# Moving the matmul operands of a transformer trunk to one address residue, and three smaller edits at its two ends

## The chip, the cores and the metric

The kernel runs on one core of one Trainium2 chip. The metric is the device time of one execution in microseconds (us). Three timed runs of the kernel before gave 1330.05, 1331.74 and 1331.91 us, median 1331.74 us.

## The reference

One layer of a hybrid encoder on 256 tokens of width 2048, all in float32:

```python
def reference(x, ...):                                   # x (1, 256, 2048)
    h = rms_norm(x, norm_mix); proj = h @ w_in            # (256, 9216): uv | q,k,v | two gates
    y_a = gmlp_branch(uv, ln_g, ln_b, w_s, b_s)           # u * (w_s @ layer_norm(v) + b), 8 groups
    y_b = neighbourhood_attn(q, k, v, rpb)                # 16 heads, windows of 4 rows x 16 columns
    merged = sigmoid(g_a) * (y_a @ w_branch[:1024]) + sigmoid(g_b) * (y_b @ w_branch[1024:])
    x = x + merged @ w_out
    up = rms_norm(x, norm_ffn) @ w_up                     # (256, 2 * 5504)
    up = conv3_over_tokens(up, conv_k) + conv_b
    gate, val = split(up)
    x = x + (silu(gate) * val) @ w_down
    return rms_norm(x, norm_final)
```

Almost all of the work is in five products with weights: `w_in`, `w_branch`, `w_out`, `w_up`, `w_down`.

## The kernel before

**Products in two halves.** Every float32 operand of a large product is held as two tiles of the type float32r: a high part (a rounded copy, written by ScalarE) and a low part (the rest, written by VectorE). A product is the sum of three: high x high, low x high, high x low. So one weight piece, a raw tile `wraw` of 128 x 1024, becomes a *unit*, the tiles `whi` and `wlo` (helpers `high`, L245, and `low`, L248). The activations are kept in the same way: `h` (the normalised input, later the normalised second input), `y` (the two branches), `m` (the merge), `a` and `s` (the activations of the down projection, and sums of them).

**A stream of pieces.** The weights lie in HBM in the order of use. `load` keeps up to five raw tiles under way (four slots of another shape, `start`, for the first 16 pieces, which carry 256 columns of the transposed x beside 1024 of weights). `begin(i)` is called ahead of every piece: it issues loads, lets `prepare` split pieces up to four ahead as units come free (`queue`, in order), and then runs the tasks that were put down for that piece with `at(i, f)`. Each engine works in the order in which this was written out.

**Which operand is loaded and which streams.** A matmul has a stationary operand (128 columns, put in by a weight load, the rows on PEld) and a moving one. There are four kinds of step:

- `first_step` (L381 to L384), the first 16 pieces: activations stationary, 512 columns of weights moving.
- `nat_step` (L364 to L366, through `three_products`): the same, for `va`, the gates, the branches and `w_out`.
- `wide_step` (L364 to L366): the down projection, 1024 columns a piece. Of its tiles three pairs in each group go through seven products in place of eight (sums of weights, made on VectorE, L301 to L304).
- `ws_step`, "ws" for weight-stationary (`spread_products`, L349 and L355), for u, q/k and the up projection: the weights are stationary. With a high weight tile, 512 columns move (both halves of 256 tokens, L349); with a low one, 256 columns (the high half alone, L355). Even pieces take highs and then lows, odd pieces lows and then highs, so that on TensorE runs of 16 highs and 16 lows alternate.

**Where tiles lie.** Pools on the left side of a partition's memory are stacked from the bottom: `const`, then `weights` (raw tiles, units 0 to 3), `tmp`, `hT` (the `h` tiles) and pools of a stage. Pools on the right are stacked from the top: `y`, the second input `x`, and `seven`, which adds units 4 and 5 and a half unit once the out projection has begun. All these tiles are multiples of 256 bytes long, so each side has one residue of its addresses modulo 256. As the kernel is built, that is 0 on the left and 224 on the right. Taking each large matmul's moving operand against the stationary operand of the next matmul in the program, 3346 of the 512-column float32r matmuls have the same residue, and 1329 differ by 32 bytes modulo 256 (the highs of units 4 and 5 in the up projection; all steps with `y`; the down steps whose weights lie in unit 4, unit 5 or the half unit). Of the 256-column ones, the lows of `ws_step`, 1304 have the same residue and 455 differ so.

**The start.** `load` is called ahead of the load of `gmix`, the scale of the first norm. Piece 0 comes in three transfers: its x columns on ScalarE's queue, its two weight halves on SP's. TensorE runs 14 transposes of an identity (`keep_awake`, L561), until the first data are there.

**The end.** In the last down group, `by_block` is 4: the four last pieces are multiplied block by block at the group's last step, so that the four blocks of the output end one after the other. The sums of the seven-product pairs are combined by `combine`, in the three tasks `one`, `two` and `three` at the pieces i + 1, i + 2 and i + 3 after the last pair.

Of the kernel before, what the change touches and what calls it, by code (L numbers as in the profile page):

```python
# [8 lines left out]
F32 = mybir.dt.float32  # L9
F32R = mybir.dt.float32r  # L10
# [5 lines left out]
T = 256  # L16
D = 2048
NT = T // 128
KD = D // 128
# [20 lines left out]
BLOCK = 1024  # L40
AHEAD = 5
RAW, UNITS, HALVES = 5, (4, 2), 1
WAKE = 14
EARLY = 4

FF_BLOCKS = ((0, 22), (22, 43))
FF_SEVEN = ((3, 5, 7), (2, 4, 6))
# [71 lines left out]
def weight_pieces():  # L119

    groups, order = weight_stream()
    out, count, at = [], {}, 0
    for key in order:
        _, w, pieces = groups[key]
        tiles, blocks = pieces[count.get(key, 0)]
        count[key] = count.get(key, 0) + 1
        cols = sum(n for _, n in blocks)
        out.append((key, w, tiles, blocks, at, cols))
        at += 128 * len(tiles) * cols
    return out, at  # L130
# [19 lines left out]
def trunk_kernel(ctx, tc, x, weights, vectors, ln_g, ln_b, w_s_turned, b_s, rpb, norm_final, out):  # L150
    nc = tc.nc
# [18 lines left out]
    ypool, y_st = pool("yT", "right")  # L170

    junk = tmp.tile([128, 512], F32, name="junk")

    banks = {n: None for n in range(8)}
    spare = list(range(8))

    def bank():
        n = spare.pop(0)
        banks[n] = psum.tile([128, 512], F32, name=f"bank{n}")
        return banks[n]  # L180
# [7 lines left out]
    pieces, _ = weight_pieces()  # L188
    kinds = {key: g[0] for key, g in weight_stream()[0].items()}
# [16 lines left out]
    def at(i, f):  # L206
        tasks.setdefault(i, []).append(f)
# [5 lines left out]
    def load():  # L213
        while n_loaded[0] < len(pieces):
            i = n_loaded[0]
            slots = start_free if i < KD else raw_free
            if not slots:
                return
            n_loaded[0] += 1
            for f in preload.pop(i, ()):  # L220
                f()
            _, _, tiles, _, off, cols = pieces[i]
            size = len(tiles) * cols
            slot = slots.pop(0)
            w = slot[0].tile([128, size if i < KD else BLOCK], F32, name=slot[1])
            for c0, c1 in ((T, 768), (0, T), (768, 1280)) if i == 0 else ((0, size),):
                queue = nc.scalar if (i, c0) == (0, 0) else nc.sync
                queue.dma_start(w[:, c0:c1], bass.AP(tensor=weights.tensor, offset=weights.offset + off + c0,
                                                       ap=[[size, 128], [1, c1 - c0]]))
            raw[i] = (w, slot)  # L230

    def raw_done(i):
        (start_free if i < KD else raw_free).append(raw.pop(i)[1])

    def unit(key):
        slot = unit_free.pop(0)
        h, l = (slot[0].tile([128, BLOCK], F32R, name=f"w{p}{slot[1]}") for p in ("hi", "lo"))
        units[key] = (h, l, slot)
        return h, l

    def unit_done(key):
        unit_free.append(units.pop(key)[2])

    def high(h, w):
        nc.scalar.activation(h, w, AF.Copy)  # L245

    def low(l, w, h):
        nc.vector.tensor_sub(l, w, h.bitcast(F32))  # L248

    def split_first(i):  # L250
        def go():
# [6 lines left out]
            else:  # L258
                nc.scalar.activation(dst[:, 0, :], x, AF.Copy, scale=g)
            nc.vector.scalar_tensor_tensor(dst[:, 1, :], x, g, dst[:, 0, :].bitcast(F32), op0=OP.mult,  # L260
                                           op1=OP.subtract)
            parts = ((0, 512), (512, 1024)) if i < EARLY else ((0, 1024),)
            for c0, c1 in parts:
# [5 lines left out]
    def split_piece(i):  # L269
        if i < KD:  # L270
            return split_first(i)

        def go():
            size = len(pieces[i][2]) * pieces[i][5]
            h, l = unit(i)
            w = raw[i][0]
            high(h[:, :size], w[:, :size])
            low(l[:, :size], w[:, :size], h[:, :size])
            raw_done(i)
        return go  # L280
# [38 lines left out]
    queue = []  # L319
# [104 lines left out]
    def wide_step(key, acts, sevens, rest, done, by_block=0):  # L424


        n0, size = starts[key], size_of[key]
        tiles = [pieces[n0 + n][2][0] for n in range(size)]
        firsts = [n for n in range(size) if n0 + n in seven]
        box, opened, left = {}, set(), {}  # L430
        OUT = {(0, 0): 2, (0, 1): 3, (1, 0): 4, (1, 1): 8}
        uses = []
        n = 0
        while n < size:
            if n in firsts:
# [12 lines left out]

        def product(u, x, w):
            start = u not in opened  # L450
            opened.add(u)
            left[u] -= 1
            three_products(p(u), x, w, start, left[u] == 0)

        def combine(i):

            nu, nv = (fx["p"].tile([128, 512], F32, name=f"comb{n}") for n in range(2))

            def one():
                nc.scalar.activation(nu, p(1), AF.Copy)  # L460
                rest(0, 0, nu, OP.add)
                nc.vector.tensor_sub(nu, nu, p(6))
                nc.vector.tensor_sub(nv, nu, p(7))
                free(p(1), p(6), p(7))

            def two():
                rest(0, 1, nu, OP.subtract)
                rest(0, 1, p(5), OP.add)
                rest(1, 0, nv, OP.add)

            def three():
                rest(1, 1, nv, OP.subtract)
                rest(1, 1, p(5), OP.add)
                free(p(5))

            for n, f in enumerate((one, two, three)):
                at(i + 1 + n, f)

        def step(i):
            n = i - n0  # L480
            c0, c1 = slice(0, 512), slice(512, 1024)
            if n in firsts:
                k = tiles[n]
                h, l, _ = halves[i]
                hb, lb, _ = units[i, "b"]
                product(1, acts(k, 0), (h, l))
                product(2, acts(k + 1, 0), (hb[:, c0], lb[:, c0]))
                product(3, sevens(k)[3], (hb[:, c1], lb[:, c1]))
                half_free.append(halves.pop(i)[2])
                unit_done((i, "b"))  # L490
            elif n - 1 in firsts:
                k = tiles[n - 1]
                ht, lt, _ = units[i - 1, "t"]
                hs, ls, _ = units[i - 1, "s"]
                S = sevens(k)
                product(5, S[0], (ht[:, c0], lt[:, c0]))
                product(7, S[2], (ht[:, c1], lt[:, c1]))
                unit_done((i - 1, "t"))
                product(6, S[1], (hs[:, c1], ls[:, c1]))
                product(4, acts(k + 1, 1), (hs[:, c0], ls[:, c0]))  # L500
                unit_done((i - 1, "s"))
                if n - 1 == firsts[-1]:
                    combine(i)
            elif n < size - by_block:
                h, l, _ = units[i]
                for (b, c), u in OUT.items():
                    cs = slice(c * 512, (c + 1) * 512)
                    product(u, acts(tiles[n], b), (h[:, cs], l[:, cs]))
                unit_done(i)
            elif n == size - 1:  # L510
                for b, c in ((0, 0), (1, 0), (0, 1), (1, 1)):
                    u = OUT[b, c]
                    for m in range(size - by_block, size):
                        h, l, _ = units[n0 + m]
                        cs = slice(c * 512, (c + 1) * 512)
                        product(u, acts(tiles[m], b), (h[:, cs], l[:, cs]))
                    done(p(u), b, c, i + 1)
                    free(p(u))
                for m in range(size - by_block, size):
# [24 lines left out]
    vec = const.tile([128, 2 * KD + 8 * NF], F32)  # L544
    gmix, gffn = vec[:, :KD], vec[:, KD:2 * KD]
    ck = vec[:, 2 * KD:].rearrange("p (j f) -> p j f", j=4)
    load()
    nc.scalar.dma_start(gmix, vectors[:, :KD])

    one = const.tile([128, 1], F32)  # L550
    nc.vector.memset(one, 1.0)
# [10 lines left out]

    keep_awake(WAKE)
    free(wake)
# [588 lines left out]
    for n in range(len(FF_BLOCKS)):  # L1153
        for j in range(2):
            key = ("down", n, j)
# [110 lines left out]
    for i, piece in enumerate(pieces):  # L1266
        key = piece[0]
# [45 lines left out]
```

## Time and profile before

| what | value |
|---|---|
| median of three timed runs | 1331.74 us |
| the profiled execution, its own time | 1331.57 us |
| span of its instructions | 1329.1 us |
| mean granted TensorE clock | 0.998 |
| TensorE busy | 1316.1 us, 99% of the span |
| VectorE busy | 71% |
| ScalarE busy | 55% |
| HBM traffic over the span | 194 GB/s |

A row of the page's groups gives the line, engine and operation, the tiles written and read without their numbers, the count, the busy time and the mean duration of one. Durations of matmuls overlap (a matmul is under way while the one before it drains), so the pace is read from the distance of two starts in the timeline, and the mean durations serve only to compare one group with another. In the timeline a row is the start, the time to the end, and what was run; "x16" are sixteen instructions of one kind in a row.

### The profile page before, as it was taken

The page shows a single profiled execution, that of the slowest core. Times are in us where ns is not written, and L with a number is a line of the kernel's source. Part 1 is how long each engine was busy: PE and PEld are TensorE (multiplying, and loading weights), DVE is VectorE, ACT ScalarE, POOL GpSimd, SP SyncE. Part 2 cuts the span into 40 slices and gives each one's busy share as a digit, 9 for nine tenths or more (in the row PEclk, how much of TensorE's full clock was granted, in tenths as well). Part 3 has the DMA queues.
Part 4 walks back from the last instruction along what each step waited for, and adds up shares of the span by engine and source line. Part 5 has one row for each costly group of instructions (what it writes and reads, how often), then busy time and mean ns, then how long its engine had stood idle before and what let it go on. Part 6 is the DMA issues. An engine that isn't in the chain of part 4 may idle for free.

```text
span 1329.1 us, 18475 instructions
## 1 busy us (share of the span) xinstructions
PE 1316.1 (99%) x6778; PEld 1116.5 (84%) x6778; DVE 945.4 (71%) x1362; ACT 728.8 (55%) x1072; POOL 100.3 (8%) x192
## 2 busy tenths in 40 slices
PE   9999999999999999999999999999999999999996
PEld 7888888888788888888888888888888888888885
DVE  5676667776564546565878777797858787869986
ACT  5855567576444444454655555554545555546553
POOL 0502065430000000000000000000000000000000
PEclk9999999999999999999999999999999999999999
DMA  8857676655556667665565656556656565546743
GB/s 327 321 177 208 195 218 191 203 151 190 180 182 189 190 189 255 204 189 187 171 203 174 200 179 199 180 175 220 207 190 190 191 187 194 183 135 222 249 147 127
DMA packets 73898, 261.40 MB, mean 197 GB/s; under 512 B 9552, under 2 KB 10832, under 8 KB 73296
## 3 DMA queue, kind: packets, MB, share of 16 engines
q1 hardware_dynamic: 69696, 252.33, 59.0%
q0 software_dynamic: 3680, 7.30, 2.0%
q8 instruction: 53, 0.87, 0.3%
q10 hardware_dynamic: 432, 0.60, 0.1%
q14 instruction: 37, 0.30, 0.1%
HBM read 256.00 MB, written 2.10 MB: 194 GB/s over the span
## 4 chain that ended last, share of the span: by engine, by line
PE 95%; DVE 3%; DMA 1%; ACT 1%; issue 0%; ACTq 0%; DVEq 0%
PE bank L349 30%; PE bank L355 16%; PE bank L364 14%; PE bank L366 14%; PE bank L365 14%; PE bank L381 1%; PE bank L382 1%; PE bank L384 1%; DVE wlo L248 1%; DMA wraw<-in_weights_dram 1%; PE bank L830 1%; ACT whi L245 0%; PE bank L882 0%; DMA vec<-in_vectors_dram 0%; PE bank L704 0%
## 5 line engine op out<-in xcount | busy, mean ns | idle before, releaser
L248 DVE TENSOR_TENSOR wlo<-wraw,whi 128x1024 fp32r<-128x1024 f32 (+1 forms) x466 | 561.2, 1217 | 231.1 <-ACT whi L245 223.5
L245 ACT ACTIVATE whi<-wraw 128x1024 fp32r<-128x1024 f32 (+1 forms) x466 | 481.1, 1046 | 285.2 <-PE bank L365 168.9
L349 PE MATMUL bank<-h,whi 128*128 128x512 f32 x1760 | 425.8, 392 | 0.0
L349 PEld LDWEIGHTS bank<-h,whi 128*128 128x128 f32 x1760 | 322.2, 188 | 64.1
L355 PEld LDWEIGHTS bank<-h,wlo 128*128 128x128 f32 x1760 | 225.3, 190 | 9.4
L355 PE MATMUL bank<-h,wlo 128*128 128x256 f32 x1760 | 229.5, 282 | 0.0
L364 PE MATMUL bank<-whi,h 128*128 128x512 f32 x320 | 126.0, 394 | 0.0
L366 PE MATMUL bank<-wlo,h 128*128 128x512 f32 x320 | 124.8, 390 | 0.0
L365 PE MATMUL bank<-whi,h 128*128 128x512 f32 x320 | 124.6, 389 | 0.0
L366 PE MATMUL bank<-wlo,a 128*128 128x512 f32 x248 | 97.2, 392 | 0.8 <-DVE wlo L248 0.8
L364 PE MATMUL bank<-whi,a 128*128 128x512 f32 x248 | 97.2, 392 | 0.0
L365 PE MATMUL bank<-whi,a 128*128 128x512 f32 x248 | 97.2, 392 | 0.0
L1020 ACT ACTIVATE tc<-ta,vec 128x256 f32<-128x256 f32 x86 | 47.1, 595 | 84.4 <-DVE ta L1018 84.4
L696 DVE TENSOR_TENSOR ta<-bank,tb 128x256 f32<-128x256 f32 x110 | 39.0, 417 | 67.6 <-ACT tb L694 67.6
L694 ACT ACTIVATE tb<-bank 128x256 f32<-128x256 f32 x110 | 36.2, 384 | 90.9 <-PE bank L349 86.2
L366 PEld LDWEIGHTS bank<-wlo,h 128*128 128x128 f32 x320 | 60.1, 188 | 12.8
L364 PEld LDWEIGHTS bank<-whi,h 128*128 128x128 f32 x320 | 60.1, 188 | 12.3
L365 PEld LDWEIGHTS bank<-whi,h 128*128 128x128 f32 x320 | 60.1, 188 | 12.0
L366 PEld LDWEIGHTS bank<-wlo,a 128*128 128x128 f32 x248 | 46.6, 188 | 11.6 <-DVE wlo L248 1.3
L364 PEld LDWEIGHTS bank<-whi,a 128*128 128x128 f32 x248 | 46.6, 188 | 10.3
L365 PEld LDWEIGHTS bank<-whi,a 128*128 128x128 f32 x248 | 46.6, 188 | 10.3
L1260 POOL DMA_DIRECT2D h<-in_norm_final_dram x4 | 2.2, 539 | 680.0 <-DVE wlo L248 679.5
(182 smaller groups left out, 1465.8 us busy)
## 6 DMA issues: line engine op xcount, KB each, us to landing
wraw<-in_weights_dram SPq DMA_DIRECT2D x446, 512.0 KB, 4.3
start<-in_weights_dram SPq DMA_DIRECT2D x15, 640.0 KB, 6.5
xs<-in_x_dram SPq DMA_DIRECT2D x2, 1024.0 KB, 9.5
vw<-va POOLq DMA_DIRECT2D x32, 64.0 KB, 5.3
x<-in_x_dram POOLq DMA_DIRECT2D x2, 1024.0 KB, 9.3
wraw<-in_weights_dram SPq DMA_DIRECT2D x8, 256.0 KB, 2.9
run<-in_rpb_dram POOLq DMA_DIRECT2D x64, 31.2 KB, 4.2
out_dram<-x SPq DMA_DIRECT2D x5, 256.0 KB, 2.8
```

The costliest lines, as they stand in the source:

```text
L245: nc.scalar.activation(h, w, AF.Copy)
L248: nc.vector.tensor_sub(l, w, h.bitcast(F32))
L349: nc.tensor.matmul(p, h[:, c:c + 128], acts(2 * n + k), start=n == 0 and k == 0, stop=last and k == tiles - 1)
L355: nc.tensor.matmul(p[:, :T], l[:, c:c + 128], acts(2 * n + k)[:, 0, :], start=False, stop=False)
L364: nc.tensor.matmul(p, xh, wh, start=start, stop=False)
L365: nc.tensor.matmul(p, xl, wh, start=False, stop=False)
L366: nc.tensor.matmul(p, xh, wl, start=False, stop=stop)
L381: nc.tensor.matmul(p, xh, h[:, cs], start=n == 0, stop=False)
L382: nc.tensor.matmul(p, xl, h[:, cs], start=False, stop=False)
L694: nc.scalar.activation(t, p[:, T:], AF.Copy)
L696: nc.vector.tensor_add(a, p[:, :T], t)
L1020: nc.scalar.activation(v, u, AF.Identity, scale=ck[:, 1, ch:ch + 1], bias=ck[:, 3, ch:ch + 1])
```

## The change

- A tile `line` of 56 floats (224 bytes) is added to `const`. It is never written or read; it moves all left pools up by 224 bytes.
- The tile `wlo` of a unit is 64 floats longer. In the weight-stationary steps the low part begins 8 floats (32 bytes) into it, in the others at its start.
- As built, all the operands of the large products lie at 224 modulo 256, and the lows of the weight-stationary steps at 0. Of the 512-column matmuls 4562 now have the same residue as the next stationary operand and 113 differ by 32 bytes; of the 256-column ones 120 and 1639. Because of the longer `wlo`, the residues modulo 512 are now mixed: 2318 of the 512-column matmuls have a stationary operand of their own that lies 256 bytes off modulo 512. Before there was no such pair.
- The load of `gmix` is issued ahead of `load`. Pieces 0, 1 and 2 come in two transfers each, columns 0 to 768 (x and the first weight half) and 768 to 1280, all on SP's queue.
- 18 transposes instead of 14 at the start.
- In the group with `by_block` the three tasks of `combine` run together at piece i + 3.

```diff
-WAKE = 14
+WAKE = 18
 EARLY = 4
+SPLIT = 3
+LINE = 64
+LOW_AT = 8
...
+    const.tile([128, 56], F32, name="line")
...
-            for c0, c1 in ((T, 768), (0, T), (768, 1280)) if i == 0 else ((0, size),):
-                queue = nc.scalar if (i, c0) == (0, 0) else nc.sync
-                queue.dma_start(w[:, c0:c1], ...)
+            for c0, c1 in ((0, 768), (768, 1280)) if i < SPLIT else ((0, size),):
+                nc.sync.dma_start(w[:, c0:c1], ...)
...
-    def unit(key):
+    def unit(key, low_at=0):
         slot = unit_free.pop(0)
-        h, l = (slot[0].tile([128, BLOCK], F32R, name=f"w{p}{slot[1]}") for p in ("hi", "lo"))
+        h = slot[0].tile([128, BLOCK], F32R, name=f"whi{slot[1]}")
+        l = slot[0].tile([128, BLOCK + LINE], F32R, name=f"wlo{slot[1]}")[:, low_at:low_at + BLOCK]
...
-            size = len(pieces[i][2]) * pieces[i][5]
-            h, l = unit(i)
+            size, key = len(pieces[i][2]) * pieces[i][5], pieces[i][0]
+            h, l = unit(i, LOW_AT if kinds[key] == "ws" else 0)
...
-                at(i + 1 + n, f)
+                at(i + 3 if by_block else i + 1 + n, f)
...
-    load()
     nc.scalar.dma_start(gmix, vectors[:, :KD])
+    load()
```

The order of TensorE's instructions is the same but for the four transposes. Two places move. On SP's queue, at the very start, these stood before (`start` are the raw tiles of the first pieces; 128x512 are the two weight halves of piece 0):

```order
L228 DMA start_86<-in_weights_dram 128x512 x2
L228 DMA start_90<-in_weights_dram 128x1280
L228 DMA start_92<-in_weights_dram 128x1280
L228 DMA start_94<-in_weights_dram 128x1280
L228 DMA start_205<-in_weights_dram 128x1280
```

and these stand there now:

```order
L231 DMA start_88<-in_weights_dram 128x768
L231 DMA start_88<-in_weights_dram 128x512
L231 DMA start_91<-in_weights_dram 128x768
L231 DMA start_91<-in_weights_dram 128x512
L231 DMA start_94<-in_weights_dram 128x768
L231 DMA start_94<-in_weights_dram 128x512
L231 DMA start_97<-in_weights_dram 128x1280
```

The x columns of piece 0 have come over from ScalarE's queue, and the first three pieces are six transfers. On VectorE, in the last down group, from the low part of the third-last piece on, these stood before (`x` is the residual that takes the result, `comb` the scratch tiles of `combine`):

```order
L248 TENSOR_TENSOR wlo_12126<-wraw_12072,whi_12125 128x1024
L958 TENSOR_TENSOR x_4961<-x_4961,comb_12123 128x512
L462 TENSOR_TENSOR comb_12123<-comb_12123,bank_11962 128x512
L463 TENSOR_TENSOR comb_12124<-comb_12123,bank_11958 128x512
L248 TENSOR_TENSOR wlo_12146<-wraw_12074,whi_12145 128x1024
L958 TENSOR_TENSOR x_4961<-x_4961,comb_12123 128x512
L958 TENSOR_TENSOR x_4961<-x_4961,bank_11954 128x512
L958 TENSOR_TENSOR x_4961<-x_4961,comb_12124 128x512
L248 TENSOR_TENSOR wlo_12165<-wraw_12092,whi_12164 128x1024
L958 TENSOR_TENSOR x_4961<-x_4961,comb_12124 128x512
L958 TENSOR_TENSOR x_4961<-x_4961,bank_11954 128x512
L964 TENSOR_TENSOR x_4961<-bank_11848,x_4961 128x512
```

and these stand there now:

```order
L252 TENSOR_TENSOR wlo_12132<-wraw_12078,whi_12131 128x1024
L252 TENSOR_TENSOR wlo_12148<-wraw_12080,whi_12147 128x1024
L252 TENSOR_TENSOR wlo_12164<-wraw_12098,whi_12163 128x1024
L962 TENSOR_TENSOR x_4967<-x_4967,comb_12129 128x512
L466 TENSOR_TENSOR comb_12129<-comb_12129,bank_11968 128x512
L467 TENSOR_TENSOR comb_12130<-comb_12129,bank_11964 128x512
L962 TENSOR_TENSOR x_4967<-x_4967,comb_12129 128x512
L962 TENSOR_TENSOR x_4967<-x_4967,bank_11960 128x512
L962 TENSOR_TENSOR x_4967<-x_4967,comb_12130 128x512 x2
L962 TENSOR_TENSOR x_4967<-x_4967,bank_11960 128x512
L968 TENSOR_TENSOR x_4967<-bank_11854,x_4967 128x512
```

The low parts of the last two pieces now stand ahead of all eight operations of `combine`, where they stood among them. ScalarE's copy for `combine` (L460) moves behind the high parts of these pieces in the same way.

More of the change, by code (lines that the diff above doesn't have):

```diff
@@ L225, in load @@
             w = slot[0].tile([128, size if i < KD else BLOCK], F32, name=slot[1])
-            for c0, c1 in ((T, 768), (0, T), (768, 1280)) if i == 0 else ((0, size),):
-                queue = nc.scalar if (i, c0) == (0, 0) else nc.sync
-                queue.dma_start(w[:, c0:c1], bass.AP(tensor=weights.tensor, offset=weights.offset + off + c0,
+            for c0, c1 in ((0, 768), (768, 1280)) if i < SPLIT else ((0, size),):
+                nc.sync.dma_start(w[:, c0:c1], bass.AP(tensor=weights.tensor, offset=weights.offset + off + c0,
                                                        ap=[[size, 128], [1, c1 - c0]]))
@@ L546, in trunk_kernel @@
     ck = vec[:, 2 * KD:].rearrange("p (j f) -> p j f", j=4)
+    nc.scalar.dma_start(gmix, vectors[:, :KD])
     load()
-    nc.scalar.dma_start(gmix, vectors[:, :KD])
     one = const.tile([128, 1], F32)
```

## The prediction

> **What bounds the kernel now.** The page's head and busy times come first, then the chain of work that ended last.
>
> ```profile
> span 1329.1 us, 18475 instructions
> PE 1316.1 (99%) x6778; PEld 1116.5 (84%) x6778; DVE 945.4 (71%) x1362; ACT 728.8 (55%) x1072; POOL 100.3 (8%) x192
> ...
> PE 95%; DVE 3%; DMA 1%; ACT 1%; issue 0%; ACTq 0%; DVEq 0%
> ```
>
> TensorE (PE) is busy 99% of the span and carries 95% of the chain. So the time is the number of matmuls times their pace, and only what changes the pace, or lies at the start and the end, can count. The pace hangs on where the operands lie. In the window from 390 to 450 us the groups by line have products with `h` (left, both operands at residue 0) beside products with `y` (right, at 224); the last two figures but one are busy time and mean duration in ns:
>
> ```profile
> L365 PE MATMUL bank<-whi,h 128*128 128x512 f32 x55 | 21.4, 389 | 0.0
> L364 PE MATMUL bank<-whi,y 128*128 128x512 f32 x32 | 12.6, 395 | 0.0
> ```
>
> In a down step the sides are exchanged (activations left, weights left or right). The timeline of the last group: piece 15 lies in a left unit, piece 16, from about 1304.3, in a right one.
>
> ```profile
> 1301.80 0.39 PE L365 MATMUL bank<-whi,a 128*128 128x512 f32 x1
> ...
> 1304.52 0.40 PE L365 MATMUL bank<-whi,a 128*128 128x512 f32 x1
> ...
> 1307.32 0.40 PE L365 MATMUL bank<-whi,a 128*128 128x512 f32 x1
> ```
>
> By the distance of starts twelve matmuls take 2.72 us, then twelve take 2.80: 226.7 and 233.3 ns. The third place is the up projection, where only the unit changes within one group:
>
> ```profile
> 702.42 3.82 PE L349 MATMUL bank<-h,whi 128*128 128x512 f32 x16
> 706.08 2.05 PE L355 MATMUL bank<-h,wlo 128*128 128x256 f32 x16
> 707.96 3.90 PE L349 MATMUL bank<-h,whi 128*128 128x512 f32 x16
> 711.70 2.06 PE L355 MATMUL bank<-h,wlo 128*128 128x256 f32 x16
> 713.59 3.82 PE L349 MATMUL bank<-h,whi 128*128 128x512 f32 x16
> 717.24 2.08 PE L355 MATMUL bank<-h,wlo 128*128 128x256 f32 x16
> 719.16 3.82 PE L349 MATMUL bank<-h,whi 128*128 128x512 f32 x16
> ```
>
> The highs at 702.42 and 713.59 are in units 0 to 3 and take 3.66 and 3.65 us by their starts; those at 707.96 are in units 4 and 5 and take 3.74. For the lows it is the other way round: 16 in left units take 1.92 us (717.24 to 719.16); where 8 of the 16 are in a right unit, 1.88 and 1.89. So 32 bytes between the moving operand and the loaded one cost a 512-column matmul 5 to 7 ns, and save a 256-column one some 3 ns (0.025 us for 8, taking 1.91 for the sixteen). The change takes the first away and spreads the second.
>
> **The sum, part by part**, against the profiled execution: 1331.57 us, of which 1329.1 is the span; that is 0.17 us under the median shown.
>
> *Gates, branches, out and down (L364 to L366).* Mixed today are 384 matmuls with `y` (4 column blocks x 2 branches x 8 tiles x 2 token blocks x 3) and 480 in right units. At 226.7 for 233.3 ns that would be 5.7 us; by the mean durations (6 ns) 5.2. I take **-5.4**.
>
> *Up projection.* Six pieces, one turn through the six units, last 719.16 - 702.42 = 16.74 us. After: highs 3.66 three times, plus 6 ns each for the last high of a run, since a low unit is loaded next; lows with all 16 off by 32 bytes: 16 save 0.05 less the last one, 1.865. Three times 5.53 is 16.59. The 176 pieces are 29.3 turns of 0.15: **-4.4**.
>
> *u and q/k.* All four units there are at 0. 48 pieces are 24 pairs, of which each gains 0.047 and pays 0.006: **-1.0**.
>
> *The end.* PE waits in the last group for the low part of the last piece, which stands behind six of the eight operations of `combine`:
>
> ```profile
> 1303.02 1.23 DVE L248 TENSOR_TENSOR wlo<-wraw,whi 128x1024 fp32r<-128x1024 f32 x1 [1.08 <-ACT whi L245]
> ...
> 1309.34 1.22 DVE L248 TENSOR_TENSOR wlo<-wraw,whi 128x1024 fp32r<-128x1024 f32 x1
> ...
> 1311.80 0.68 DVE L964 TENSOR_TENSOR x<-bank,x 128x512 f32<-128x512 f32 x1
> ```
> ```profile
> 1309.38 0.39 PE L365 MATMUL bank<-whi,a 128*128 128x512 f32 x1
> 1310.61 0.50 PE L366 MATMUL bank<-wlo,a 128*128 128x512 f32 x1 [0.84 <-DVE wlo L248]
> 1310.95 0.39 PE L364 MATMUL bank<-whi,a 128*128 128x512 f32 x1
> ```
>
> 1.23 + 0.34 us stand where 0.46 would do: 1.1 us of stall. Between the low at 1303.0 and this one stand six operations and one more low. Moved, the six come behind, three lows run from 1303.0 on at 1.2 us each, and the last is done near 1306.6, ahead of its use by over 2 us. Queued behind them is L964, which takes the first block; VectorE (DVE) ends `combine` near 1311.5, as today, so L964 starts as today, some 1.5 us after its block, and the next block is 2.7 us later. Nothing is late next: **-1.1**.
>
> *The start.*
>
> ```profile
> 1.37 3.25 PE L561 MATMUL bank<-ident 128*128 128x128 f32 x14 [1.37 <-POOL ident masks.py:199]
> 5.60 0.77 PE L381 MATMUL bank<-whi,h 128*128 128x512 f32 x1 [0.98 <-DVE h L257]
> ...
> 9.18 0.63 PE L381 MATMUL bank<-whi,h 128*128 128x512 f32 x1
> 9.61 0.46 PE L382 MATMUL bank<-whi,h 128*128 128x512 f32 x1
> 9.91 0.62 PE L384 MATMUL bank<-wlo,h 128*128 128x512 f32 x2
> 10.37 0.39 PE L381 MATMUL bank<-whi,h 128*128 128x512 f32 x1
> ```
> ```profile
> 5.10 0.35 DVE L257 TENSOR_SCALAR h<-start,vec 128x256 fp32r<-128x256 f32 x1 [4.22 <-DMA vec<-in_vectors_dram]
> ...
> 8.24 0.51 ACT L259 ACTIVATE h<-start,vec 128x256 fp32r<-128x256 f32 x1 [2.81 <-DMA start<-in_weights_dram]
> ```
>
> The first product waits for L257, and that for `gmix` (`vec`). With `gmix` ahead, that wait ends earlier; if it gains the 0.4 us or more that one issue takes, the transposes bind instead: by the page's row 14 of them fill 3.25 us, four more take it to about 5.3, against 5.60. The twelve products of piece 0 run at 0.43 us until 9.7 and at 0.23 from there. The pace doubles 4.1 us after PE began to work without a gap. After the change there is no gap from 1.37 on; if the transposes count as work, the same 4.1 us are over at 5.5. One execution doesn't tell how fixed that time is, so I put it at 6.3. With 2.4 slow products, piece 0 ends at 5.3 + 1.0 + 9.6 x 0.227 = 8.5 instead of 10.37. Piece 1 has to be there: it landed by 8.24 as a whole, and its first 60% now land alone, near 7; 0.5 + 0.6 us of ScalarE (ACT) work make it 8.2. So -2.2 at the best, -0.3 if the transposes don't count. SP's two issues more hide behind the wait for the first landing. I take **-1.5**, nearer the row of a busy PE, and keep both ends.
>
> The Trainium skill ("TensorE: Matmul & The Clock Gate", Part 4: PE-mode transpose) says that transposes don't count as PE work in the same way and leave the clock low. By it the sum would hold -0.3 here. The trace does not contradict it: 3.25 us of transposes raised nothing by 9.2.
>
> *What may give back.* Around the seven-product pairs DVE is the nearest to binding:
>
> ```profile
> 1250.00:1260.00 10.00, 10.00 (x45) 8.15 (x45) 9.93 (x12) 5.24 (x5) 0.00 (x0) 1.00 0.69 232
> ```
>
> In this stretch DVE is busy 9.93 of 10 us (the figure ahead of x12). A PE that is quicker by 0.7 us in each of four down groups may meet it: 0 to 0.6, I take **+0.2**. Loads into tiles at 224 cost nothing: 1024 KB of x land in 9.5 us at residue 0 (`xs`) and in 9.3 at 224 (`x`).
>
> ```profile
> xs<-in_x_dram SPq DMA_DIRECT2D x2, 1024.0 KB, 9.5
> ...
> x<-in_x_dram POOLq DMA_DIRECT2D x2, 1024.0 KB, 9.3
> ```
>
> Together -5.4 - 4.4 - 1.0 - 1.1 - 1.5 + 0.2 = -13.2, so **1318.4 us**.
>
> **The rivals.**
>
> *A distance of 256 bytes is not a distance of nothing.* The longer `wlo` puts 2318 of the 512-column pairs 256 bytes apart modulo 512, and no row of before has such a pair. The rows show that multiples of 512 are harmless (the columns of one tile) and that 32 bytes on either side cost the same. If 256 bytes cost 6.2 ns too, 2430 matmuls are slow instead of 1329: +6.8, less 3.5 for the lows, less 2.4 at the ends: 1332.5, no change. For it: nothing but the gap in the rows.
>
> *Each operand's own residue costs, not the distance* (the other side). Every slow row today has one operand off 0; after, all 4675 have. Then 3346 more pay 6.2 ns: +20.7 - 3.5 - 2.4 = 1346.4, slower. It decides as soon as a run of 16 highs with both at 224 reads 3.90 and not 3.82. Against it: the price is the same whichever operand is off, and a mere misplacement should not make the lows quicker.
>
> *The lows lose.* Seen are lows whose stationary operand is 32 bytes below; now it is 32 above. For highs both signs cost the same; for lows this one is not shown. Without their gain (4.5 with u and q/k) 1322 to 1323; if they lose 3 ns, 1327.
>
> *The residue does nothing*, the rows differing by the stage. Then only the ends count: 1329.2. The Trainium skill speaks for it ("TensorE: Matmul & The Clock Gate", Part 2: What happens when you issue a matmul): the two operands have read ports of their own, and loading weights takes nothing from the running matmul. The up rows speak against it: same line, same stage, 3.66 and 3.74 us.
>
> **How the numbers follow.** Forecast 0.72; distance of 256 bytes 0.08; own residue 0.05; lows 0.09; nothing 0.04; the rest 0.02, on either side. What two measurements can tell apart is about 0.2%, 2.7 us. Faster is the forecast, the lows, most of "nothing" and a little of the rest: 0.86; within 0.2% 0.08; slower 0.06. The forecast's own range: residue -9.5 to -12, end -1.0 to -1.3, start -0.3 to -2.2, DVE 0 to +0.6, so 1316 to 1321.4; half a us lower for what the start's pace does from one execution to the next, and up into the lows' case: 1315.5 to 1323.5.
>
> **What would show it.** In the timeline, highs of every up pair at 3.82 (3.66 by starts) and lows at 1.86 to 1.87; L364 to L366 at 389 ns with `y` and `a` alike; no stall of PE in the last group; the first product at 5.3 and piece 1 before 9. Wrong would be 3.90 everywhere, paces that change with the unit, or lows of 1.91 and more.

## The result, and the profile after

| | us |
|---|---|
| before, median of 6 runs | 1331.57 (1330.05 to 1331.91) |
| after, median of 6 runs | 1322.01 (1321.42 to 1322.55) |
| ratio | 0.993, 95% interval 0.9917 to 0.9943 |
| profiled execution, before and after | 1331.57 and 1321.85 |
| their spans | 1329.1 and 1319.4 |

The change is faster by 9.6 us. The forecast was 13.2. The time lies inside the stated range, but only because that range reached up into the place of a rival: the one on the lows of the weight-stationary steps had 1322 to 1323. The head of the page after, its busy times and the shares of its chain of waits:

```profile
span 1319.4 us, 18485 instructions
...
PE 1307.8 (99%) x6782; PEld 1114.7 (84%) x6782; DVE 945.5 (72%) x1362; ACT 728.8 (55%) x1072; POOL 100.1 (8%) x192
...
PE 97%; DVE 2%; DMA 1%; ACT 0%; issue 0%; POOL 0%; DVEq 0%; ACTq 0%; POOLq 0%
```

TensorE is still the bound, with 8.3 us less of busy time. Which groups lost it is seen in the groups by line of TensorE, before (busy us, then mean ns of one):

```profile
L349 PE MATMUL bank<-h,whi 128*128 128x512 f32 x1760 | 425.8, 392 | 0.0
L355 PE MATMUL bank<-h,wlo 128*128 128x256 f32 x1760 | 229.5, 282 | 0.0
...
L364 PE MATMUL bank<-whi,a 128*128 128x512 f32 x248 | 97.2, 392 | 0.0
...
L364 PE MATMUL bank<-whi,y 128*128 128x512 f32 x128 | 50.7, 396 | 0.0
```

and after (every line number is 4 higher):

```profile
L353 PE MATMUL bank<-h,whi 128*128 128x512 f32 x1760 | 426.2, 393 | 0.0
L359 PE MATMUL bank<-h,wlo 128*128 128x256 f32 x1760 | 228.4, 281 | 0.0
...
L368 PE MATMUL bank<-whi,a 128*128 128x512 f32 x248 | 96.5, 389 | 0.0
...
L368 PE MATMUL bank<-whi,y 128*128 128x512 f32 x128 | 50.0, 391 | 0.0
```

The products with `y` and `a` are down to 389 to 391 ns, as forecast. The first two rows, those of the weight-stationary steps, are where they were: 655.3 us together before, 654.6 after.

A finer account comes from the starts of the same matmul in both traces, counted from the last one. The change is ahead by 2.5 us from the second piece on (7.90 for 10.37), still by 2.5 after u and q/k, by 5.8 at the end of gates, branches and out, by 6.0 after the first up half, 7.5 after the first down half, 7.6 after the second up half, and 10.2 at the last matmul. From there to the end of the span it loses 0.5.

| stretch | forecast | measured |
|---|---|---|
| L364 to L366 (gates, branches, out, both down halves less the stall) | -5.4 | -6.1 |
| up projection, u, q/k | -5.4 | -0.5 |
| the start | -1.5 | -2.5 |
| the end: stall of TensorE / tail behind the last matmul | -1.1 / 0 | -1.1 / +0.5 |
| VectorE | +0.2 | 0 |

Here are the timelines of the end: TensorE's last matmul before and after, and what VectorE does around it.

```profile
1318.95 0.39 PE L366 MATMUL bank<-wlo,a 128*128 128x512 f32 x1
```
```profile
1308.79 0.39 PE L370 MATMUL bank<-wlo,a 128*128 128x512 f32 x1
```
```profile
1316.63 0.69 DVE L1098 TENSOR_TENSOR x<-bank,x 128x512 f32<-128x512 f32 x1 [0.86 <-PE bank L366]
...
1319.38 0.68 DVE L1098 TENSOR_TENSOR x<-bank,x 128x512 f32<-128x512 f32 x1
```
```profile
1298.19 0.68 DVE L962 TENSOR_TENSOR x<-x,comb 128x512 f32<-128x512 f32 x1
...
1303.49 0.68 DVE L968 TENSOR_TENSOR x<-bank,x 128x512 f32<-128x512 f32 x1
...
1307.02 0.68 DVE L1102 TENSOR_TENSOR x<-bank,x 128x512 f32<-128x512 f32 x1
...
1309.76 0.68 DVE L1102 TENSOR_TENSOR x<-bank,x 128x512 f32<-128x512 f32 x1
```

Before, VectorE waited 0.86 us for TensorE at the third block, and took the last block 0.43 us after the last matmul's start. After, it comes to the third block (1307.02) with no wait for TensorE, and takes the last one 0.97 us after the last matmul's start. TensorE no longer stalls, and VectorE is what is late.

### The profile page after: what moved, and what is told of

Same layout as the page of the kernel before. It is cut to its first block, busy times and chain, and to the rows that moved or that the text cites. A ratio compares the mean times of both kernels' runs of the same rounds, so it can differ in the third digit from the quotient of the medians.

```text
span 1319.4 us, 18485 instructions
## 1 busy us (share of the span) xinstructions
PE 1307.8 (99%) x6782; PEld 1114.7 (84%) x6782; DVE 945.5 (72%) x1362; ACT 728.8 (55%) x1072; POOL 100.1 (8%) x192
## 4 chain that ended last, share of the span: by engine, by line
PE 97%; DVE 2%; DMA 1%; ACT 0%; issue 0%; POOL 0%; DVEq 0%; ACTq 0%; POOLq 0%
PE bank L353 31%; PE bank L359 16%; PE bank L368 15%; PE bank L370 15%; PE bank L369 15%; PE bank L386 1%; PE bank L385 1%; PE bank L388 1%; DMA wraw<-in_weights_dram 1%; PE bank L834 1%; DVE wlo L252 0%; PE bank L886 0%; DVE x L962 0%; PE bank L565 0%; PE bank L708 0%; PE bank L995 0%
## 5 line engine op out<-in xcount | busy, mean ns | idle before, releaser
L368 PE MATMUL bank<-whi,h 128*128 128x512 f32 x320 | 126.0, 394 | 0.0
L370 PE MATMUL bank<-wlo,h 128*128 128x512 f32 x320 | 124.7, 390 | 0.0
L370 PE MATMUL bank<-wlo,a 128*128 128x512 f32 x248 | 96.6, 389 | 0.0
L368 PE MATMUL bank<-whi,a 128*128 128x512 f32 x248 | 96.5, 389 | 0.0
L370 PEld LDWEIGHTS bank<-wlo,h 128*128 128x128 f32 x320 | 60.0, 188 | 12.7
L368 PEld LDWEIGHTS bank<-whi,h 128*128 128x128 f32 x320 | 60.1, 188 | 12.3
L370 PEld LDWEIGHTS bank<-wlo,a 128*128 128x128 f32 x248 | 46.5, 188 | 9.9 <-DVE wlo L252 0.3
L368 PEld LDWEIGHTS bank<-whi,a 128*128 128x128 f32 x248 | 46.6, 188 | 9.6
```

The costliest lines, as they stand in the source:

```text
L368: nc.tensor.matmul(p, xh, wh, start=start, stop=False)
L370: nc.tensor.matmul(p, xh, wl, start=False, stop=stop)
```

## The experiments

Each starts from the changed kernel. Unless something else is said, four runs or more stand behind a time.

### Placement: which part pays

**Residue undone.** Left pools and lows go back to 0 modulo 256; start and end stay changed.

```diff
-    const.tile([128, 56], F32, name="line")
-LOW_AT = 8
+LOW_AT = 0
```

> The changed kernel without the tile line and with the lows at the start of their tile: the residues are those of before (left 0, right 224), start and end stay changed. If the residue matters for the products with activations stationary (864 mixed matmuls at 6 to 7 ns, 5.5 to 6.0 us) and almost nothing for the weight-stationary steps (16.74 us for six up pieces in the trace of before, 16.72 after: 0.5 us over the stage), this gives 1322.0 + 6.3 = 1328.3 us. If the weight-stationary steps gained the 5.4 us that were forecast and lost them to something else in the change, it gives up to 1333. If the residue does nothing, 1322. In the trace, products with y back at 395 ns and the up highs of units 4 and 5 back at 3.74 us a run.

Measured 1328.0 us (1327.73 to 1329.11), 0.9975 of before [0.9965, 0.9985]. In its groups the row of `a` is back at 392 ns:

```profile
L367 PE MATMUL bank<-whi,a 128*128 128x512 f32 x248 | 97.2, 392 | 0.0
```

(The line numbers of this run are one lower than those of the change.) So placement is worth 6 us, and start and end together 3.6.

**Lows level.** One residue for everything, without the offset of the lows.

```diff
-LOW_AT = 8
+LOW_AT = 0
```

> The changed kernel with the lows at 224 like everything else. Theory: what the lows gain by the 32 bytes (1.91 to 1.89 us a run of 16) the highs behind them pay back (3.65 to 3.68), so a pair of runs takes 5.57 us either way and the time is 1321.5 to 1322.5. Rival, the step as forecast: the lows' offset saves 0.04 us a pair over 112 pairs and the highs are late for another reason; then the time is 1326 and a pair takes 5.61. In the trace of the theory: runs of highs at 3.65, of lows at 1.91.

Measured 1321.93 us (1321.47 to 1322.34): no different from the change. The offset of 32 bytes above is worth nothing. From residue undone to the change, by the starts of the same matmuls, 5.8 us arise in L368 to L370 and 0.5 in the weight-stationary steps.

**Lows below.** The low part begins 56 floats in: at 192 modulo 256, 32 bytes below the moving operand and not above it.

```diff
-LOW_AT = 8
+LOW_AT = 56
```

> The changed kernel with the lows of the weight-stationary steps at 192 modulo 256, 32 bytes below their moving operand, as they stood in the right units of before. Theory: the sign does not matter, what the lows gain the highs pay back, a pair of runs takes 5.57 us and the time is 1321.5 to 1322.5. Rival, the one named in the forecast (lows that are loaded from 32 bytes below gain 3 ns, from above not): pairs of 5.53 us and 1317.5.

Measured 1317.1 us (1316.45 to 1317.51), 0.9889 of before [0.9872, 0.9905]. My theory of that moment, that the sign does not matter, fell; its rival held. Three timelines of the up projection show it: 32 bytes above (the change), level, and 32 bytes below. The last row of each starts one turn of three pairs after the first.

```profile
690.90 3.84 PE L353 MATMUL bank<-h,whi 128*128 128x512 f32 x16
694.58 2.05 PE L359 MATMUL bank<-h,wlo 128*128 128x256 f32 x16
696.47 3.84 PE L353 MATMUL bank<-h,whi 128*128 128x512 f32 x16
...
707.62 3.84 PE L353 MATMUL bank<-h,whi 128*128 128x512 f32 x16
```
```profile
691.62 3.82 PE L353 MATMUL bank<-h,whi 128*128 128x512 f32 x16
695.27 2.08 PE L359 MATMUL bank<-h,wlo 128*128 128x256 f32 x16
697.19 3.82 PE L353 MATMUL bank<-h,whi 128*128 128x512 f32 x16
...
708.32 3.82 PE L353 MATMUL bank<-h,whi 128*128 128x512 f32 x16
```
```profile
690.09 3.82 PE L353 MATMUL bank<-h,whi 128*128 128x512 f32 x16
693.75 2.03 PE L359 MATMUL bank<-h,wlo 128*128 128x256 f32 x16
695.62 3.82 PE L353 MATMUL bank<-h,whi 128*128 128x512 f32 x16
...
706.67 3.82 PE L353 MATMUL bank<-h,whi 128*128 128x512 f32 x16
```

By starts, 16 highs and 16 lows take 3.68 + 1.89 = 5.57 us above, 3.65 + 1.92 = 5.57 level, and 3.66 + 1.87 = 5.53 below. Above, the lows gain half of what the forecast gave them and the highs that follow lose it. Below, a turn is 16.58 us; the forecast for the change was 16.59, the change has 16.72. With 1760 / 16 = 110 pairs of runs, 0.045 us each are 5.0 us, and 1322.01 - 1317.1 is 4.9.

**Sweep.** A kernel, executed once, in which each column group of the gates, each quarter of the out projection and each group of up pieces has its own offset in its unit.

```diff
-    def unit(key, low_at=0):
+    def unit(key, high_at=0, low_at=0):
...
-        h = slot[0].tile([128, BLOCK], F32R, name=f"whi{slot[1]}")
+        h = slot[0].tile([128, BLOCK + LINE], F32R, name=f"whi{slot[1]}")[:, high_at:high_at + BLOCK]
...
-            h, l = unit(i, LOW_AT if kinds[key] == "ws" else 0)
+            h, l = unit(i, *shifts(key))
```

> The changed kernel with another distance between the operands in each group, by an offset of the weights inside their tile. Gates and out (weights moving): 16, 32, 48, 64, 96, 128, 160, 192 bytes (gates 0,0; 1,0; 0,1; 1,1; 0,2; 1,2; 0,3; 1,3), 224, 240, 8 and 256 bytes (out 0 to 3). Up groups (weights stationary): high and low by pairs of such offsets. Theory (distance modulo 256): 32, 224 cost 6 to 7 ns a 512-column matmul, 256 costs nothing, and the curve is the same on both sides of 128. Rival (only an exact match of the 256-byte residue is quick): all but 256 cost the same 6 to 7 ns. Rival (each operand's own place costs): the curve is not symmetric. In the up groups both highs and lows off by 32 bytes give 5.62 us or more a pair, lows alone 5.57. The time as a whole decides nothing here, some 3 to 8 us above the changed kernel.

It took 1329.24 us. The mean distance of starts in L383 to L385 (L368 to L370 of the change), by the address of the next stationary operand less that of the moving one, modulo 256; some 90 pairs each, 1738 at 0, starts more than 250 ns apart left out:

| bytes | -128 | -96 | -64 | -48 | -32 | -16 | -8 | 0 | +16 | +32 | +64 | +96 |
|---|---|---|---|---|---|---|---|---|---|---|---|---|
| ns | 232 | 233 | 229 | 233 | 233 | 232 | 234 | **227** | 236 | 233 | 233 | 234 |

Only 0 is quick; -64 lies between. The rival "only an exact match" is nearly right: distance does not matter, being level does. For the weight-stationary steps, the sum of 16 highs and 16 lows in ns, by the offset of highs and of lows against the moving operand (ten of the nineteen pairs tried; the other nine lie between 5567 and 5633):

| highs, lows | -64, -64 | 0, -32 | 0, -16 | 0, +96 | 0, +64 | +64, +64 | 0, 0 | 0, +32 | +32, +32 | -32, 0 |
|---|---|---|---|---|---|---|---|---|---|---|
| sum | 5520 | 5526 | 5527 | 5534 | 5540 | 5548 | 5567 | 5573 | 5627 | 5641 |

Three places in the timeline: highs level with lows 32 below, both 64 above, and both 64 below:

```profile
801.73 2.03 PE L374 MATMUL bank<-h,wlo 128*128 128x256 f32 x16
803.59 3.82 PE L368 MATMUL bank<-h,whi 128*128 128x512 f32 x16
807.26 2.03 PE L374 MATMUL bank<-h,wlo 128*128 128x256 f32 x16
...
1023.36 1.98 PE L374 MATMUL bank<-h,wlo 128*128 128x256 f32 x16
1025.18 3.89 PE L368 MATMUL bank<-h,whi 128*128 128x512 f32 x16
1028.91 1.98 PE L374 MATMUL bank<-h,wlo 128*128 128x256 f32 x16
...
1113.02 1.98 PE L374 MATMUL bank<-h,wlo 128*128 128x256 f32 x16
1114.83 3.82 PE L368 MATMUL bank<-h,whi 128*128 128x512 f32 x16
1118.49 2.05 PE L374 MATMUL bank<-h,wlo 128*128 128x256 f32 x16
1120.38 3.84 PE L368 MATMUL bank<-h,whi 128*128 128x512 f32 x16
```

With both 64 above, the lows take only 1.82 us, but the highs, at 3.73, are among the slowest. With both 64 below, runs of lows take 1.81 and 1.89 us in turn, although as built they all have the same addresses modulo 512. That whole group of eight pieces takes 22.07 us, against 22.12 with lows 32 below and 22.11 with lows 16 below. So no offset tried beats these two by more than 0.2%; at +16 (5567) and at the change's +32 nothing is gained.

### The start

**Start undone** (14 transposes, the old order and split of the loads), **loads undone** (the old loads, 18 transposes) and **14 transposes** (with the new loads). The edit shown is that of the first; the second has it without its first two lines, the third has these two alone.

```diff
-WAKE = 18
+WAKE = 14
...
-            for c0, c1 in ((0, 768), (768, 1280)) if i < SPLIT else ((0, size),):
+            for c0, c1 in ((T, 768), (0, T), (768, 1280)) if i == 0 else ((0, size),):
...
-    nc.scalar.dma_start(gmix, vectors[:, :KD])
     load()
+    nc.scalar.dma_start(gmix, vectors[:, :KD])
```

> The changed kernel with the start of before: piece 0 in three transfers, gmix behind them, 14 transposes. Theory: the start gave 2.5 us in the two profiled executions (the second piece begins at 7.90 instead of 10.37), of which up to 1.5 hang on when the clock rises; so 1324 to 1325, and the first product back at 5.6. Rival: the start gave only the 0.3 of the case in which transposes do not count, and the rest was the luck of one execution: 1322.0 to 1322.6.

> The changed kernel with the loads of before (piece 0 in three transfers, gmix behind them, pieces 1 and 2 whole), but 18 transposes. With 14 transposes these loads gave 1324.6 and the new loads 1324.2. Theory: the two parts need each other; with 18 transposes the clock is up early, but the second piece then waits for its data until 9.3 as with the old loads, so 1323.3 to 1323.9. Rival: the four transposes alone bring it all, 1322.0 to 1322.6.

> The changed kernel with 14 transposes instead of 18, gmix and the split loads kept. The first product can then start at 4.9 (ScalarE's first high part and gmix bind it), after a gap of 0.4 us, and in one execution in several the clock rises one window later. Theory: the start's 2.6 us come mostly from the loads, since the second piece waits for its data (9.34 with the old loads although the clock was up at 6.0), so 1322.0 to 1322.8. Rival: the gap ahead of the first product keeps the clock low until about 9, and the time goes to 1323.5 or more.

| | 14 transposes | 18 transposes |
|---|---|---|
| old loads | 1324.62 (1324.23 to 1325.01) | 1323.53 (1323.07 to 1323.69) |
| new loads | 1324.18 (1323.08 to 1325.02) | 1322.01 (1321.42 to 1322.55) |

The loads are worth 1.5 us beside 18 transposes, as expected of that run; beside 14 the two times can't be told apart. The transposes were expected to be worth next to nothing beside the new loads and are worth 2.2: my theory missed. The starts in TensorE's timeline, of the change and with the loads undone (line numbers one higher):

```profile
1.37 3.79 PE L565 MATMUL bank<-ident 128*128 128x128 f32 x18 [1.37 <-POOL ident masks.py:199]
4.92 0.48 PE L385 MATMUL bank<-whi,h 128*128 128x512 f32 x1
5.26 0.50 PE L386 MATMUL bank<-whi,h 128*128 128x512 f32 x1
5.59 0.40 PE L385 MATMUL bank<-whi,h 128*128 128x512 f32 x1
5.83 0.40 PE L386 MATMUL bank<-whi,h 128*128 128x512 f32 x1
...
7.90 0.39 PE L385 MATMUL bank<-whi,h 128*128 128x512 f32 x1
```
```profile
5.51 0.47 PE L386 MATMUL bank<-whi,h 128*128 128x512 f32 x1 [0.38 <-DVE h L262]
...
9.30 0.50 PE L386 MATMUL bank<-whi,h 128*128 128x512 f32 x1 [0.54 <-ACT whi L250]
```

In the change the products run at full pace (0.24 us from start to start) from 5.6 on, 0.7 us after the first of them. With the old loads piece 1 is late (9.30, a wait for its high part), and a quick first piece is worth nothing.

How much the start gains differs between executions, because the clock rises at another time in each. In the eight profiles with 18 transposes and the new loads it rose at 4.2 to 7.1 us, and the second piece began at 7.89 to 8.88, in the mean 8.26. With the whole start of before (the profile of before and two of start undone) the piece began at 9.34 to 10.37, in the mean 9.87. So the 2.5 us between the change and before set one of the earliest of its kind against the latest of the other; the means are 1.6 apart.

**Second profiles** of start undone and of 14 transposes, one execution each, to see where their time goes.

> The same kernel as in the run with the whole start undone, for a second profile. In the first profile 1.57 us of its distance to the changed kernel arose in the first two pieces, and 1.0 us in one stall of TensorE near 1280 us, ahead of a low matmul of the seven-product pairs, after a raw piece that landed late (ScalarE waited 2.60 us for it, against 1.38). Theory (the later start shifts the loads, and the stall belongs to this kernel): the stall of 0.6 to 1.1 us is there again at the same place, first products from 5.5 to 5.6, second piece 9.3 to 10.4. Rival (the landing scatters from execution to execution): no stall over 0.3 us near 1280, and a time of 1323.2 to 1323.8 if the clock rises near 6 us, up to 1324.6 if it rises later.

> The same kernel as in the run with 14 transposes and the new loads, for a second profile; in the first the clock rose at 6.7 us and the second piece began at 8.53, where the changed kernel has 4.7 and 7.90, while three of its four times lay 0.6 to 1.9 us above the profiled one. Theory (with 14 transposes the rise falls anywhere from 6 to 10 us, and that is the spread): the rise again later than 6 us, the second piece at 8.3 to 9.9, and the time follows it one for one: 1322.9 plus what the second piece lies behind 8.3, within 0.4 us. Rival (the spread has another source): the second piece within 0.2 us of 8.53 while the time is over 1323.6, or a stall elsewhere.

They took 1325.72 and 1323.78 us. With 14 transposes and the new loads the second piece began at 8.23, only 0.33 us behind the change; so the late clock was not the source, my theory fell, and the rival's "stall elsewhere" held. It is in the last down group, in TensorE's timeline:

```profile
1277.78 0.50 PE L368 MATMUL bank<-whi,s 128*128 128x512 f32 x1 [0.32 <-ACT whi L249]
...
1279.19 0.50 PE L370 MATMUL bank<-wlo,s 128*128 128x512 f32 x1 [0.68 <-DVE wlo L252]
```

The same two waits stand in the second profile of start undone (0.33 and 0.69), the second one also in its first. Counted from start to start they cost 1.0 to 1.6 us in three of the four profiles with 14 transposes and the changed addresses, 0.5, spread over the group, in the fourth. None of the nine profiles with 18 transposes has one there. Behind them is a raw piece that lands late. ScalarE's timeline, in the second profile of 14 transposes and in the change:

```profile
1272.90 1.06 ACT L249 ACTIVATE whi<-wraw 128x1024 fp32r<-128x1024 f32 x1 [3.12 <-DMA wraw<-in_weights_dram]
```
```profile
1270.91 1.06 ACT L249 ACTIVATE whi<-wraw 128x1024 fp32r<-128x1024 f32 x1 [1.38 <-DMA wraw<-in_weights_dram]
```

In all five profiles with 14 transposes, the one of before too, this wait is 2.2 to 3.1 us; in all nine with 18 it is 1.1 to 1.4. The DMA view of the window from 1266 to 1272 us says what else is on the engines, again 14 transposes and then the change:

```profile
q1 hardware_dynamic: 250, 0.93, 51.6%
q8 instruction: 1, 0.02, 1.8%
```
```profile
q1 hardware_dynamic: 289, 1.08, 60.8%
```

With 14 transposes a fetch of instructions, one packet of 16 KB that occupies its DMA engine for 1.2 to 2.0 us, starts 1.0 to 2.5 us after the issue of this piece, among its packets. With 18 it starts 2.8 to 2.9 us ahead of the issue and is over. That holds for all fourteen profiles. So what the four transposes are seen to do is to shift the instruction stream, so that a fetch does not meet a piece that is waited for. That they gain anything at the start itself, beside the new loads, is not shown: with 14 of them the second piece began at 8.53 and 8.23, within the spread of the eight profiles with 18. That the fetch is the cause of the late landing, and not only always there, is argued and not shown either: no run moved it by itself.

### The end

**Combine undone**: the three tasks at i + 1, i + 2 and i + 3 again. **Combine split**: the first at i + 1, the others at i + 3.

```diff
-                at(i + 3 if by_block else i + 1 + n, f)
+                at(i + 1 + n, f)
```

> The changed kernel with one, two and three at i + 1, i + 2 and i + 3 as before. Theory: the stall of 1.1 to 1.3 us for the last low part comes back, and the 0.5 us by which VectorE now trails TensorE at the very end goes away (the last eviction started 0.43 us after the last matmul's start before, 0.97 after): 1322.0 + 0.7 = 1322.7. Rival: the tail's 0.5 us have another cause, then 1323.2. Rival: with the faster pace the stall does not return, 1321.5.

```diff
-                at(i + 3 if by_block else i + 1 + n, f)
+                at(i + 3 if by_block and n else i + 1 + n, f)
```

> The changed kernel with task one of combine at i + 1 as before, two and three at i + 3. VectorE then does the first three operations while it waits for the last pieces' transfers, and reaches the first block's eviction earlier; the last low part is still ahead of its use. Theory (the 0.5 us of tail lost to VectorE's late start on the blocks): last eviction 0.45 to 0.7 us after the last matmul instead of 0.97, 1321.5 to 1321.8. Rival: the last low part comes late again and PE waits, 1322.3 or more.

Undone: 1322.46 us (1322.31 to 1324.82). The stall is back in TensorE's timeline:

```profile
1301.93 0.50 PE L370 MATMUL bank<-wlo,a 128*128 128x512 f32 x1 [1.02 <-DVE wlo L252]
```

but the tail behind the last matmul's start is 10.2 us, as before (10.2), where the change has 10.6. Split: 1321.33 us (1321.21 to 1321.67), no stall, tail 10.1. VectorE waits for TensorE again at the third block:

```profile
1302.45 0.68 DVE L968 TENSOR_TENSOR x<-bank,x 128x512 f32<-128x512 f32 x1
...
1306.68 0.69 DVE L1102 TENSOR_TENSOR x<-bank,x 128x512 f32<-128x512 f32 x1 [0.62 <-PE bank L370]
```

So the change took 1.1 us of stall away and gave 0.5 back, in profiles where VectorE trails. It does not always: with all three tasks at i + 3 the tail is 10.1 to 11.0 us in ten profiles, with the first at i + 1 it is 10.1 to 10.2 in four.

### The two together

**Best**: lows 32 below and combine split.

```diff
-LOW_AT = 8
+LOW_AT = 56
...
-                at(i + 3 if by_block else i + 1 + n, f)
+                at(i + 3 if by_block and n else i + 1 + n, f)
```

> The changed kernel with both edits that gained: the lows of the weight-stationary steps 32 bytes below their moving operand (offset 56 floats), and combine's first task at i + 1, the others at i + 3. If the two are independent, 1317.1 - 0.7 = 1316.4 us, pairs of runs at 5.53 us and the last eviction 0.5 us after the last matmul. If a quicker PE brings back a wait for the last low parts, 1317 or more.

Measured 1317.32 us (1316.67 to 1318.35), 0.9897 of before [0.9881, 0.9914]. It is faster than the change by 4.7 us and not to be told from lows below alone (1317.1). The 1316.4 us expected of two independent gains were missed by 0.9, and the reason given for that case did not show: its trace has no wait of TensorE for the last low parts. Its span, 1314.6 us in the profiled run, contains a clock that rose only at 6.3 us, where that of lows below rose at 4.7; what the split saves is no larger than that spread.

## Why the prediction was right, and where it was wrong

- **What bounds.** Right: 97% of the chain is TensorE, and only pace, start and end moved the time.
- **L364 to L366** (L368 to L370 after the change). Right, and a little low: -6.1 by starts, -5.6 by the busy times of the groups, for -5.4. The mechanism, equal residues of the moving operand and the next stationary one, was shown by taking it away (1328.0 for 1321.93 us) and by the sweep.
- **Up projection, u and q/k.** This is the step that failed: "lows with all 16 off by 32 bytes: 16 save 0.05". The 0.05 was read from rows where the lows lay 32 bytes *below* the moving operand; the change puts them 32 *above*. The rival on the lows said that this sign was not shown and gave 1322 to 1323 us. With it the two terms came to -0.5 us where -4.4 and -1.0 were forecast. Lows below show that the size was right for the other sign: 16.58 us a turn for the forecast 16.59, and 1317.1 us for the whole, below the forecast of 1318.4. The chance of 0.09 was too small for the one sign that no row showed, with a term of 4.5 us on it, and the range held the result only by reaching into this rival's case.
- **The start.** Right mechanism, -2.5 for -1.5 in these two executions. The clock was put up at 6.3 us and was up at 4.7 in this one; piece 1 was there. The extra 1 us is luck: by the means of eight and of three profiles the second piece came 1.6 us earlier. The lower end, -0.3, stood for transposes that do not count as work. The Trainium skill ("TensorE: Matmul & The Clock Gate", Part 4: PE-mode transpose) says that they don't and leave the clock low. This trace contradicts it: TensorE had run nothing but transposes from 1.37 to 4.92 us, the record of the granted clock has it up at 4.71, the last transposes already came 0.11 us apart where they had come 0.21 apart, and the third product ran at full pace.
- **The end.** "Nothing is late next" was wrong. L964 was said to start as today; but as VectorE gets through `combine` later against TensorE, it is itself late by the third block, and 0.5 of the 1.1 us comes back.
- **VectorE in the seven-product pairs** (0 to +0.6, taken +0.2). Not there in the change. It was not far off: with 14 transposes a late piece in just this stretch stalls TensorE by up to 1.6 us.
- **The rivals that fell.** A distance of 256 bytes is harmless: in the trace of the change, the matmuls of L368 to L370 and of the first pieces take 226.9 ns with 256 bytes modulo 512 between the two operands (some 1400 pairs) and 227.0 with none (some 1470). An operand's own residue costs nothing: highs with both operands at 224 take 3.65 us where the lows are level too, as with both at 0 before. And residue does something, 6 us. The read ports of their own of which the Trainium skill tells ("TensorE: Matmul & The Clock Gate", Part 2: What happens when you issue a matmul) do not describe what these rows show: 227 or 233 ns, by where the next operand to be loaded lies.

## What to carry to other kernels

A price read from rows holds for the sign and the side at which they stand: if a change mirrors a distance, the mirrored case is unmeasured, and a sweep of one constant in one kernel costs a single run. Where TensorE binds at 99%, try putting the moving operand and the next stationary operand of 512-column matmuls at the same address modulo 256 bytes, and the stationary operand of 256-column runs 16 or 32 bytes below; here that was worth 6 and 5 us of 1331, and only this kernel shows it. After an edit that adds a few instructions, look for what moved with the instruction stream before crediting the instructions themselves.

## What the runs showed of the hardware

- The pace of float32r matmuls depends on addresses: 227 ns at 512 columns when the next stationary operand is level with the moving one modulo 256 bytes, 229 to 236 at every other offset tried. At 256 columns level is not the quickest place: 16 level lows take 1.91 us, 16 that lie 32 below 1.87, 96 below or 128 away 1.92, and 16 that lie 64 above 1.82 where the highs lie there too, but 1.89 where the highs are level. Why the highs' offset matters to the lows stays open. Addresses alone do not set the pace: with both 64 below, runs of lows alternate between 1.81 and 1.89 us at the same addresses modulo 512.
- The cost can fall on another matmul. Where highs and lows are both level, the first five highs after a run of lows take 228 to 236 ns and the rest 226 to 227; after lows at +32 it is the first nine, at 224 to 236, and the last one, ahead of a low that is not level, takes 235.
- The clock can rise on transposes alone: in five of the fourteen profiles it rose, at 4.2 to 5.4 us, before the first product had begun. With 18 transposes it rose at 4.2 to 7.1 us, with 14 at 5.4 to 9.7. In every one of the profiles the record of the clock then has it up for a whole number of steps of 3.413 us (382 to 385 of them), so rise and fall lie on a grid of that step. That the rise waits for the next point of a grid that lies elsewhere in each execution fits this, but no run shows it by itself.
- An instruction fetch of 16 KB among the packets of a 512 KB load goes with that load landing 1 to 2 us later, 1270 us into the program. It fell there in all five profiles with 14 transposes at the start and in none of the nine with 18.
